# Moving two tiny per-row operations from GpSimd to VectorE in a layer norm with GELU

## The chip, the cores and the metric

The kernel runs on one core of a Trainium2 chip. The metric is the device time of that core in microseconds (us). All runs compared here are of the same state (fast, TensorE clock 1.0 in the profiles).

## The reference

```python
x: (8, 1024, 2048) float32          # 8192 rows of 2048
mean = np.mean(x, axis=-1, keepdims=True)
var = np.var(x, axis=-1, keepdims=True)
normalized = (x - mean) / np.sqrt(var + eps)
out = gamma * normalized + beta
return 0.5 * out * (1 + np.tanh(np.sqrt(2 / np.pi) * (out + 0.044715 * out ** 3)))
```

Input and output are 67.1 MB each, and each has to cross once between HBM (the memory outside the core) and SBUF (the memory that the engines work on).

## The kernel before

A row tile is 128 rows. There are 64 of them, in 16 batches of four. A batch (4.19 MB) is loaded by one DMA into one of five slots, worked on in place, and stored from the same slot by one DMA. A slot is reloaded when its store has landed. The first batch is loaded, and the last one stored, tile by tile. For each tile the engines do this:

- VectorE: four statistics instructions of 512 elements (`bn_stats`), an aggregate (`mvs` = mean and variance), and, for the tile before, the multiplication by gamma (`zg`).
- GpSimd: `ves` = variance + eps, `rss` = ves to the power -1/2, `nms` = -mean * rss.
- ScalarE: `yk` = x * rss + nms, and, for the tile before, GELU out of PSUM (the memory that TensorE sums into) back into the slot.
- TensorE: beta (two rows) plus zg, summed in PSUM.

```python
# GpSimd, per row tile k of a batch
po.tensor_scalar(out=ves[:, c], in0=mvs[:, k, 1:2], scalar1=float(eps), scalar2=1.0,
                 op0=ALU.add, op1=ALU.mult)._wait_ge(s_a, k + 1).then_inc(s_q, 1)
po.tensor_tensor(out=rss[:, c], in0=ves[:, c], in1=mhalf, op=ALU.pow)._wait_ge(s_q, 2 * k + 1).then_inc(s_q, 1)
po.tensor_scalar(out=nms[:, c], in0=mvs[:, k, 0:1], scalar1=rss[:, c], scalar2=-1.0,
                 op0=ALU.mult, op1=ALU.mult)._wait_ge(s_q, 2 * k + 2).then_inc(s_p, 1)
...
# VectorE, per row tile: stats(k), then scale(k - 1)
def stats(s, q, wait, count):
    ...                                   # four bn_stats
    ve.bn_aggr(out=mvs[:, q], in_=sts[:, q])._wait_ge(s_o, count).then_inc(s_a, 1)
def scale(q, count):
    ve.tensor_tensor(out=zgs[q % 2], in0=yks[q % 2], in1=g_t, op=ALU.mult)._wait_ge(s_n, count).then_inc(s_z, 1)
...
# ScalarE, per row tile t: yk(t), then gelu(t - 1); after a batch's last gelu its store
ac.activation(out=yks[t % 2], in_=xts[slot(b)][:, q], func=ACT.Identity, scale=rss[:, q:q + 1],
              bias=nms[:, q:q + 1])._wait_ge(s_p, t + 1).then_inc(s_n, 1)
...
# SyncE: before a slot is loaded again, its store must have landed
sy.wait_ge(s_store[s], stored(b))
```

Of the kernel before, what the change touches and what calls it, by code (L numbers as in the profile page):

```python
# [8 lines left out]
ALU = mybir.AluOpType  # L9

R = 4
SLOTS = 5
# [4 lines left out]
def kernel(  # L17
# [28 lines left out]
    def sb(name, shape, dt):  # L46
        return pool.tile(shape, dt, name=name)
# [13 lines left out]
    sts = sb("sts", [P, R, nsub, nc.vector.BN_STATS_DIM], f32)  # L61
    mvs = sb("mvs", [P, R, 2], f32)
    ves = sb("ves", [P, R], f32)
    rss = sb("rss", [P, R], f32)
    nms = sb("nms", [P, R], f32)

    def sem(name):
        return tc.alloc_semaphore(name)

    s_first = [sem(f"first{q}") for q in range(R)]  # L70
    s_load = [sem(f"load{s}") for s in range(SLOTS)]
# [4 lines left out]
    s_o = sem("o")  # L76
    s_a = sem("a")
    s_z = sem("z")
    s_q = sem("q")
    s_p = sem("p")  # L80
# [7 lines left out]
    def slot(b):  # L88
        return (b + SLOTS - 1) % SLOTS

    def row(p):
        return rows[p:p + 1, :, :d // K]

    def split(v):
        return v.rearrange("o (k f) -> o k f", k=K)
# [10 lines left out]
    with tc.tile_critical(no_gpsimd_drain=True):  # L106
        with nc.Block(no_gpsimd_drain=True) as block:

            @block.sync
            def _(sy):  # L110
                for b in range(B):
                    s = slot(b)
                    if stored(b):
                        sy.wait_ge(s_store[s], stored(b))
                    for q in range(R):
                        if b == 0:
                            sy.dma_start(out=xts[s][:, q:q + 1], in_=xg[0, :, q:q + 1]).then_inc(s_first[q], 16)
                    if b:
                        sy.dma_start(out=xts[s], in_=xg[b]).then_inc(s_load[s], 16)

            @block.gpsimd
            def _(po):
                po.memset(ones, 1.0)  # L123
                po.memset(ones_b, 1.0)
                po.memset(mhalf, -0.5)
                po.memset(ident, 0.0).then_inc(s_setp, 1)
                po.affine_select(out=ident, in_=ident, compare_op=ALU.not_equal, fill=1.0, base=0,  # L127
                                 pattern=[[-1, P]], channel_multiplier=1)._wait_ge(s_setp, 1).then_inc(s_setp, 1)
                with po.Fori(0, B):
                    for k in range(R):  # L130
                        c = slice(k, k + 1)
                        po.tensor_scalar(out=ves[:, c], in0=mvs[:, k, 1:2], scalar1=float(eps), scalar2=1.0,  # L132
                                         op0=ALU.add, op1=ALU.mult)._wait_ge(s_a, k + 1).then_inc(s_q, 1)
                        po.tensor_tensor(out=rss[:, c], in0=ves[:, c], in1=mhalf,  # L134
                                         op=ALU.pow)._wait_ge(s_q, 2 * k + 1).then_inc(s_q, 1)
                        po.tensor_scalar(out=nms[:, c], in0=mvs[:, k, 0:1], scalar1=rss[:, c], scalar2=-1.0,  # L136
                                         op0=ALU.mult, op1=ALU.mult)._wait_ge(s_q, 2 * k + 2).then_inc(s_p, 1)
                    po.sem_inc(s_a, -R)
                    po.sem_inc(s_q, -2 * R)

            @block.vector
            def _(ve):
                def stats(s, q, wait, count):
                    xr = xts[s][:, q].rearrange("p (s f) -> p s f", f=FMAX)
                    for j in range(nsub):
                        ins = ve.bn_stats(out=sts[:, q, j, :], in_=xr[:, j, :])  # L146
                        if j == 0 and wait:
                            ins._wait_ge(*wait)
                            if wait[0] is s_load[s]:
                                ins.then_inc(s_load[s], -16)  # L150
                    ins.then_inc(s_o, 1)
                    ve.bn_aggr(out=mvs[:, q], in_=sts[:, q])._wait_ge(s_o, count).then_inc(s_a, 1)  # L152

                def scale(q, count):
                    ve.tensor_tensor(out=zgs[q % 2], in0=yks[q % 2], in1=g_t,  # L155
                                     op=ALU.mult)._wait_ge(s_n, count).then_inc(s_z, 1)

                ve.memset(b_hl, 0.0).then_inc(s_m, 1)  # L158
                for q in range(R):
                    stats(slot(0), q, (s_first[q], 16), q + 1)  # L160
                    if q == 0:

                        ve.tensor_tensor(out=split(b_hl[32:33]), in0=row(32), in1=split(b_hl[32:33]),  # L163
                                         op=ALU.subtract)._wait_ge(s_c, 2).then_inc(s_m, 1)
                        ve.wait_ge(s_c, 3)
                    else:
                        scale(q - 1, q)
                ve.sem_inc(s_o, -R)
                ve.sem_inc(s_n, -(R - 1))
                with ve.Fori(0, (B - 1) // SLOTS):  # L170
                    for k in range(SLOTS * R):
                        s, q = divmod(k, R)
                        stats(s, q, (s_load[s], 16) if q == 0 else None, k + 1)
                        scale((q - 1) % R, k + 1)
                    ve.sem_inc(s_o, -SLOTS * R)
                    ve.sem_inc(s_n, -SLOTS * R)
                scale(R - 1, 1)

            @block.scalar
# [100 lines left out]
```

## Time and profile before

| | before |
|---|---|
| median time | 319.93 us (319.73 to 319.96, 3 runs) |
| span in the profile | 318.1 us |
| busy: ScalarE, VectorE, TensorE, GpSimd | 251.5, 247.1, 244.4, 110.5 us |
| DMA | 134.26 MB, mean 422 GB/s over the span |

Three compute engines are busy 77 to 79% of the span, and none is full. The view of groups gives, for the lines concerned, the count, the busy time in us and the mean duration of one in ns, then the idle time ahead of them:

```profile
L132 POOL TENSOR_SCALAR ves<-mvs 128x1 f32<-128x1 f32 x64 | 38.4, 600 | 174.1 <-DVE mvs L152 174.1
L155 DVE TENSOR_TENSOR zg<-yk,g_t 128x2048 bf16<-128x2048 bf16 x64 | 76.4, 1194 | 19.4 <-ACT yk L192 19.4
...
L136 POOL TENSOR_SCALAR nms<-mvs,rss 128x1 f32<-128x1 f32 x64 | 35.9, 560 | 6.3
L134 POOL TENSOR_TENSOR rss<-ves,mhalf 128x1 f32<-128x1 f32 x64 | 35.3, 551 | 5.3
```

The means of the first and third hide two cases each, alone and while zg runs: 0.19 and 1.03 us for the addition, 0.27 and 0.88 us for the product (the timeline in the prediction shows all but the 0.27). The idle time of 174.1 us says that GpSimd mostly waits for work. The wait of 19.4 us is VectorE's, for yk, the result that needs the GpSimd chain.

### The profile page before, as it was taken

The numbers are of one execution on the slowest core, as the hardware profiler recorded it, in microseconds if no ns is written. First come the engines' busy times: TensorE is split into PE (matmuls) and PEld (weight loads), VectorE is DVE, ScalarE is ACT, GpSimd is POOL, SyncE is SP. The second block draws the span as 40 slices with busy tenths as digits, with TensorE's granted clock in tenths as the row PEclk, the third lists the DMA queues.
The fourth block names the chain that finished last, engine by engine and source line by source line (L and its number), as shares of the span: only waits on it lengthen the run. The fifth ranks groups of instructions, "written<-read, shape, count | busy, mean of one in ns | idle before, by whom it ended". The sixth has DMA issues, their size and how long they took to land.

```text
span 318.1 us, 2087 instructions
## 1 busy us (share of the span) xinstructions
PE 244.4 (77%) x520; PEld 57.3 (18%) x520; DVE 247.1 (78%) x386; ACT 251.5 (79%) x132; POOL 110.5 (35%) x201
## 2 busy tenths in 40 slices
PE   2769999999999999997868959589595886958810
PEld 1212222222212122221112212112121111211100
DVE  3499999999999999978968699686986869778400
ACT  2669999999999999997967969599595995968820
POOL 1144444444444444443333343342432324423100
DMA  7999999999999999999999999999999999999994
GB/s 292 437 462 396 433 413 408 457 424 433 437 424 445 413 453 424 433 437 424 445 412 457 420 437 433 429 441 416 453 420 441 433 429 441 416 453 412 445 401 205
DMA packets 5570, 134.26 MB, mean 422 GB/s; under 512 B 656, under 2 KB 704, under 8 KB 704
## 3 DMA queue, kind: packets, MB, share of 16 engines
q1 hardware_dynamic: 2736, 67.11, 49.4%
q10 hardware_dynamic: 2832, 67.13, 49.0%
q14 instruction: 2, 0.02, 0.0%
HBM read 67.13 MB, written 67.11 MB: 422 GB/s over the span
## 4 chain that ended last, share of the span: by engine, by line
DMA 45%; DVE 19%; ACT 18%; POOL 9%; PE 3%; issue 2%; ACTq 0%; POOLq 0%; DVEq 0%; SPq 0%
DMA out_dram<-xt 28%; DMA xt<-in_x_dram 15%; ACT yk L192 13%; DVE sts L146 12%; DVE zg L155 5%; POOL ves L132 5%; ACT xt L199 4%; POOL rss L134 3%; PE ps L217 2%; DMA rows<-in_gamma_dram 2%; POOL nms L136 1%; DVE mvs L152 1%; PE ps L234 1%; ACT g_t L188 1%; ACTq L202 0%
## 5 line engine op out<-in xcount | busy, mean ns | idle before, releaser
L146 DVE BATCH_NORM_STATS2 sts<-xt 128x6 f32<-128x512 f32 x256 | 157.7, 678 | 29.2 <-DMA xt<-in_x_dram 27.0
L192 ACT ACTIVATE yk<-xt,nms,rss 128x2048 bf16<-128x2048 f32 x64 | 133.7, 2089 | 44.0 <-POOL nms L136 39.0
L234 PE MATMUL ps<-zg,ident 128*128 128x512 bf16 x256 | 120.8, 628 | 50.7 <-DVE zg L155 49.5
L230 PE MATMUL ps<-b_hl,ones_b 33*128 33x512 bf16 x256 | 120.6, 624 | 2.2 <-PEq L225 2.2
L199 ACT ACTIVATE xt<-ps 128x2048 f32<-128x2048 f32 x64 | 119.0, 1859 | 1.5 <-PE ps L234 1.5
L132 POOL TENSOR_SCALAR ves<-mvs 128x1 f32<-128x1 f32 x64 | 38.4, 600 | 174.1 <-DVE mvs L152 174.1
L155 DVE TENSOR_TENSOR zg<-yk,g_t 128x2048 bf16<-128x2048 bf16 x64 | 76.4, 1194 | 19.4 <-ACT yk L192 19.4
L234 PEld LDWEIGHTS ps<-zg,ident 128*128 128x128 bf16 x256 | 27.8, 131 | 143.8 <-DVE zg L155 108.5
L230 PEld LDWEIGHTS ps<-b_hl,ones_b 33*128 33x128 bf16 x256 | 27.0, 127 | 92.1 <-issue 88.4
L136 POOL TENSOR_SCALAR nms<-mvs,rss 128x1 f32<-128x1 f32 x64 | 35.9, 560 | 6.3
L134 POOL TENSOR_TENSOR rss<-ves,mhalf 128x1 f32<-128x1 f32 x64 | 35.3, 551 | 5.3
L152 DVE BATCH_NORM_AGGREGATE mvs<-sts 128x2 f32<-128x24 f32 x64 | 16.8, 263 | 2.2
L217 PE MATMUL ps<-rows,ones 1*128 1x512 f32 x8 | 7.2, 1076 | 6.0 <-DMA rows<-in_gamma_dram 6.0
L185 ACT ACTIVATE b_hl<-rows 1x2048 bf16<-1x2048 f32 x1 | 1.9, 1908 | 4.8 <-DMA rows<-in_beta_dram 4.8
L217 PEld LDWEIGHTS ps<-rows,ones 1*128 1x128 f32 x8 | 2.5, 325 | 9.1 <-DMA rows<-in_gamma_dram 6.0
L163 DVE TENSOR_TENSOR b_hl<-rows,b_hl 1x2048 bf16<-1x2048 f32 x1 | 2.3, 2281 | 2.2 <-ACT b_hl L186 2.2
L188 ACT ACTIVATE g_t<-ps 128x2048 bf16<-128x2048 f32 x1 | 1.9, 1877 | 2.5 <-PE ps L217 2.5
L181 ACT ACT_TABLE_LOAD x1 | 1.3, 1283 | 0.9 <-SPq L106 0.9
L186 ACT ACTIVATE b_hl<-rows 1x2048 bf16<-1x2048 f32 x1 | 1.9, 1908 | 0.0
L158 DVE MEMSET b_hl<- 33x1024 uint32 x1 | 0.9, 912 | 1.2 <-SPq L106 1.2
L123 POOL MEMSET ones<- 65x128 f32 x1 | 0.2, 201 | 0.5 <-SPq L106 0.5
L127 POOL TENSOR_SCALAR_AFFINE_SELECT ident<-ident 128x128 bf16<-128x128 bf16 x1 | 0.3, 294 | 0.1
(7 smaller groups left out, 0.9 us busy)
## 6 DMA issues: line engine op xcount, KB each, us to landing
xt<-in_x_dram SPq DMA_DIRECT2D x15, 4096.0 KB, 24.8
out_dram<-xt ACTq DMA_DIRECT2D x15, 4096.0 KB, 37.5
xt<-in_x_dram SPq DMA_DIRECT2D x4, 1024.0 KB, 8.2
out_dram<-xt ACTq DMA_DIRECT2D x4, 1024.0 KB, 13.1
rows<-in_beta_dram ACTq DMA_DIRECT2D x2, 8.0 KB, 5.5
rows<-in_gamma_dram ACTq DMA_DIRECT2D x1, 8.0 KB, 5.1
```

Of the source, the lines that this page charges most:

```text
L132: po.tensor_scalar(out=ves[:, c], in0=mvs[:, k, 1:2], scalar1=float(eps), scalar2=1.0, op0=ALU.add, op1=ALU.mult)._wait_ge(s_a, k + 1).the ...
L134: po.tensor_tensor(out=rss[:, c], in0=ves[:, c], in1=mhalf, op=ALU.pow)._wait_ge(s_q, 2 * k + 1).then_inc(s_q, 1)
L136: po.tensor_scalar(out=nms[:, c], in0=mvs[:, k, 0:1], scalar1=rss[:, c], scalar2=-1.0, op0=ALU.mult, op1=ALU.mult)._wait_ge(s_q, 2 * k + 2 ...
L146: ins = ve.bn_stats(out=sts[:, q, j, :], in_=xr[:, j, :])
L152: ve.bn_aggr(out=mvs[:, q], in_=sts[:, q])._wait_ge(s_o, count).then_inc(s_a, 1)
L155: ve.tensor_tensor(out=zgs[q % 2], in0=yks[q % 2], in1=g_t, op=ALU.mult)._wait_ge(s_n, count).then_inc(s_z, 1)
L188: ac.activation(out=g_t, in_=pss[0], func=ACT.Identity)._wait_ge(s_tg, 1).then_inc(s_c, 1)
L192: ac.activation(out=yks[t % 2], in_=xts[slot(b)][:, q], func=ACT.Identity, scale=rss[:, q:q + 1], bias=nms[:, q:q + 1])._wait_ge(s_p, t + ...
L199: ins = ac.activation(out=xt[:, q], in_=pss[i % 2], func=ACT.Gelu_apprx_tanh)._wait_ge(s_t, i + 1)
L217: ins = pe.matmul(pss[0][:, cols(j)], lhsT=ones[64:65], rhs=rows[64:65, j * K // nsub:(j + 1) * K // nsub, :d // K], start=True, stop=True)
L230: ins = pe.matmul(ps[:, cols(j)], lhsT=ones_b, rhs=b_hl[:, cols(j)], start=True, stop=False)
L234: ins = pe.matmul(ps[:, cols(j)], lhsT=ident, rhs=zgs[k % 2][:, cols(j)], start=False, stop=True)
```

## The change

The intent is to shorten the chain from the aggregate to yk: GpSimd keeps only the power. VectorE computes variance + eps right after the aggregate, and -mean/sigma after the first statistics instruction of the next tile, when the power should be done.

```diff
 # GpSimd
-po.tensor_scalar(out=ves[:, c], ... add eps ...)._wait_ge(s_a, k + 1).then_inc(s_q, 1)
 po.tensor_tensor(out=rss[:, c], in0=ves[:, c], in1=mhalf,
-                 op=ALU.pow)._wait_ge(s_q, 2 * k + 1).then_inc(s_q, 1)
-po.tensor_scalar(out=nms[:, c], ... -mean * rss ...)._wait_ge(s_q, 2 * k + 2).then_inc(s_p, 1)
+                 op=ALU.pow)._wait_ge(s_a, k + 1).then_inc(s_q, 1)
 # VectorE, per row tile
 for j in range(nsub):
     ins = ve.bn_stats(out=sts[:, q, j, :], in_=xr[:, j, :])
+    if j == 0 and before is not None:
+        mean(before, count_q)          # nms = -mean * rss of the tile before, waits for the power
-ve.bn_aggr(out=mvs[:, q], in_=sts[:, q])._wait_ge(s_o, count).then_inc(s_a, 1)
+ve.bn_aggr(out=mvs[:, q], in_=sts[:, q])._wait_ge(s_o, count + 1).then_inc(s_o, 1)
+ve.tensor_scalar(out=ves[:, q:q + 1], ... add eps ...)._wait_ge(s_o, count + 2).then_inc(s_a, 1)
 scale(before, ...)                    # zg of the tile before, as it was
 ... (semaphore resets adjusted; ScalarE, TensorE and SyncE unchanged)
```

More of the change, by code (lines that the diff above doesn't have):

```diff
@@ L131, in _, with mean, step @@
                         c = slice(k, k + 1)
-                        po.tensor_scalar(out=ves[:, c], in0=mvs[:, k, 1:2], scalar1=float(eps), scalar2=1.0,
-                                         op0=ALU.add, op1=ALU.mult)._wait_ge(s_a, k + 1).then_inc(s_q, 1)
                         po.tensor_tensor(out=rss[:, c], in0=ves[:, c], in1=mhalf,
-                                         op=ALU.pow)._wait_ge(s_q, 2 * k + 1).then_inc(s_q, 1)
-                        po.tensor_scalar(out=nms[:, c], in0=mvs[:, k, 0:1], scalar1=rss[:, c], scalar2=-1.0,
-                                         op0=ALU.mult, op1=ALU.mult)._wait_ge(s_q, 2 * k + 2).then_inc(s_p, 1)
+                                         op=ALU.pow)._wait_ge(s_a, k + 1).then_inc(s_q, 1)
                     po.sem_inc(s_a, -R)
-                    po.sem_inc(s_q, -2 * R)
             @block.vector
             def _(ve):
-                def stats(s, q, wait, count):
+                def mean(q, count):
+                    c = slice(q, q + 1)
+                    ve.tensor_scalar(out=nms[:, c], in0=mvs[:, q, 0:1], scalar1=rss[:, c], scalar2=-1.0,
+                                     op0=ALU.mult, op1=ALU.mult)._wait_ge(s_q, count).then_inc(s_p, 1)
+                def step(s, q, wait, count, before, count_q, count_n):
                     xr = xts[s][:, q].rearrange("p (s f) -> p s f", f=FMAX)
@@ L146, in stats @@
                         ins = ve.bn_stats(out=sts[:, q, j, :], in_=xr[:, j, :])
-                        if j == 0 and wait:
-                            ins._wait_ge(*wait)
-                            if wait[0] is s_load[s]:
-                                ins.then_inc(s_load[s], -16)
-                    ins.then_inc(s_o, 1)
-                    ve.bn_aggr(out=mvs[:, q], in_=sts[:, q])._wait_ge(s_o, count).then_inc(s_a, 1)
+                        if j == 0:
+                            if wait:
+                                ins._wait_ge(*wait)
+                                if wait[0] is s_load[s]:
+                                    ins.then_inc(s_load[s], -16)
+                            if before is not None:
+                                mean(before, count_q)
+                    ins.then_inc(s_o, 1)
+                    ve.bn_aggr(out=mvs[:, q], in_=sts[:, q])._wait_ge(s_o, count + 1).then_inc(s_o, 1)
+                    ve.tensor_scalar(out=ves[:, q:q + 1], in0=mvs[:, q, 1:2], scalar1=float(eps), scalar2=1.0,
+                                     op0=ALU.add, op1=ALU.mult)._wait_ge(s_o, count + 2).then_inc(s_a, 1)
+                    if count_n:
+                        scale(before, count_n)
                 def scale(q, count):
@@ L159, in _ @@
                 for q in range(R):
-                    stats(slot(0), q, (s_first[q], 16), q + 1)
+                    step(slot(0), q, (s_first[q], 16), 2 * q, q - 1 if q else None, q, q)
                     if q == 0:
@@ L165, in _ @@
                         ve.wait_ge(s_c, 3)
-                    else:
-                        scale(q - 1, q)
-                ve.sem_inc(s_o, -R)
+                ve.sem_inc(s_o, -2 * R)
+                ve.sem_inc(s_q, -(R - 1))
                 ve.sem_inc(s_n, -(R - 1))
@@ L172, in _ @@
                         s, q = divmod(k, R)
-                        stats(s, q, (s_load[s], 16) if q == 0 else None, k + 1)
-                        scale((q - 1) % R, k + 1)
-                    ve.sem_inc(s_o, -SLOTS * R)
+                        step(s, q, (s_load[s], 16) if q == 0 else None, 2 * k, (q - 1) % R, k + 1, k + 1)
+                    ve.sem_inc(s_o, -2 * SLOTS * R)
+                    ve.sem_inc(s_q, -SLOTS * R)
                     ve.sem_inc(s_n, -SLOTS * R)
+                mean(R - 1, 1)
                 scale(R - 1, 1)
```

## The prediction

VectorE's added work: the sum came to 0.27 us per tile (17 us over 64 tiles, 4.03 us a tile, 8.06 us a pair). The durations of the two new operations in it came from no run; what stands of its terms is the 0.08 us by which zg overlaps the aggregate in the trace. So these sums, and the 264 us of VectorE, are forecasts and no measurements. That yk would be there before zg's turn was forecast with the same durations. The sum on the time, 0 us, does not need these terms: it sets the pair's 8.06 or 8.19 us against 9.76 us of DMA at the measured 430 GB/s. The 0.3 us in the sum for the batch boundary agree with the trace, where the product starts 0.30 us before yk (60.80 to 61.10).

> **What bounds the kernel now.** I read the page's busy shares and slices first, because they say whether one resource is full from end to end.
>
> ```profile
> span 318.1 us, 2087 instructions
> ...
> DVE  3499999999999999978968699686986869778400
> ACT  2669999999999999997967969599595995968820
> POOL 1144444444444444443333343342432324423100
> DMA  7999999999999999999999999999999999999994
> ```
>
> Each digit is the busy tenth of a slice of 8 us. VectorE is full only up to slice 17 or so (about 135 us); after that it has holes. The DMA engines are full from the second slice to the last but one. 134.26 MB have to move, and the stretches show at what rate:
>
> ```profile
> 12.00:36.00 24.00, 18.38 (x40) 4.06 (x39) 20.63 (x33) 19.18 (x10) 8.39 (x14) 1.00 1.03 444
> 60.00:130.00 70.00, 63.02 (x137) 14.56 (x136) 64.63 (x104) 64.73 (x35) 30.19 (x54) 1.00 1.00 433
> 205.00:280.00 75.00, 58.67 (x128) 13.68 (x128) 58.10 (x92) 59.49 (x32) 27.23 (x48) 1.00 1.00 433
> 304.00:314.00 10.00, 0.00 (x0) 0.00 (x0) 0.00 (x0) 1.17 (x1) 0.00 (x0) 1.00 0.97 411
> ```
>
> The columns are PE, weight loads, VectorE, ScalarE and GpSimd busy, the clock, the DMA share and GB/s. The rate is 433 both while VectorE is 92% busy (64.63 of 70 us) and while it is 77% busy (58.10 of 75). So compute does not set it. Data flows from about 2 to 314 us: 134.26 MB / 312 us = 430 GB/s. [...]
>
> The second view is who waits in the load queue (SyncE):
>
> ```profile
> SPq L119 <- DMA out_dram<-xt: 246.9, 11, 55.6
> ```
>
> Every reload of a slot waits for the store of that slot. In the timeline the loads from 138 us on are issued every 19.5 us, as are the stores: one batch in and one out, 8.39 MB / 19.5 us = 430 GB/s. A store takes about 44 us from issue to landing then, of which its own data at full rate are only 4.19 MB / 430 GB/s = 9.8 us. The rest is queue. Compute sees the queue as holes: in the waits of VectorE, the statistics waited 27.0 us for loads in 9 waits. The chain of waits, which begins with 130 us of VectorE, GpSimd and ScalarE links, is misleading here. It follows one order of events back, but while it runs through compute the DMA queues have other buffers' work and never empty.
>
> [...]
>
> ```profile
> 58.86 1.16 DVE L155 TENSOR_TENSOR zg<-yk,g_t 128x2048 bf16<-128x2048 bf16 x1
> 59.03 1.03 POOL L132 TENSOR_SCALAR ves<-mvs 128x1 f32<-128x1 f32 x1 [2.63 <-DVE mvs L152]
> ...
> 62.78 0.19 POOL L132 TENSOR_SCALAR ves<-mvs 128x1 f32<-128x1 f32 x1 [1.72 <-DVE mvs L152]
> 63.06 0.55 POOL L134 TENSOR_TENSOR rss<-ves,mhalf 128x1 f32<-128x1 f32 x1
> 63.10 1.85 ACT L199 ACTIVATE xt<-ps 128x2048 f32<-128x2048 f32 x1
> 63.23 1.23 DVE L155 TENSOR_TENSOR zg<-yk,g_t 128x2048 bf16<-128x2048 bf16 x1 [0.53 <-ACT yk L192]
> 63.71 0.88 POOL L136 TENSOR_SCALAR nms<-mvs,rss 128x1 f32<-128x1 f32 x1
> ```
>
> The GpSimd addition takes 0.19 us alone and 1.03 us when the multiplication into zg runs, ending 0.04 us after it. [...]
>
> **The change part by part.** Per row tile (64 of them):
> - Removed from GpSimd: the addition (600 ns mean, 38.4 us in all) and the product (560 ns, 35.9 us). Left is the power, 35.3 us. GpSimd falls from 110.5 to some 36 us if the power never meets zg. It may well meet it, since it now starts when zg starts[...].
> - Added on VectorE: two operations of 128x1. [...] Statistics of 678 ns start every 0.59 us in their groups of four, so neighbours overlap by 0.08 to 0.09 us[...]. The addition waits for the end of the aggregate (263 ns), which today zg overlaps by 0.08 us (66.87 + 0.26 = 67.13 against a start at 67.05). [...] Sum 0.27 us per tile, 17 us over 64 tiles: VectorE goes from 247.1 to about 264 us busy, 83% of the span.
> - The step of compute: today two tiles take 8.19 us (zg starts at 58.86 and 67.05), one step of 3.76 and one of 4.43 us, the longer with a wait of 0.53 us for yk, which came late through three GpSimd operations. With 0.27 added VectorE's own work is 3.76 + 0.27 = 4.03 us a tile. [...] That wait goes. So 8.06 instead of 8.19 us per pair: compute gains 1 to 2% at best.
> - What lies on the path of the end: nothing of this. A tile is 1.05 MB in and 1.05 MB out, so a pair of tiles needs 4.19 MB / 430 GB/s = 9.76 us of DMA. Both 8.06 and 8.19 are below it.
> - The batch boundary: the product of a batch's last tile now stands behind the first statistics of the next batch, so it waits for that load. zg of that tile already stood behind all four statistics, so the store comes only some 0.1 to 0.4 us later: yk is ready at landing + 0.6 + 0.3 + 2.1 = 3.0 us and zg starts then, against 2.7 us today (279.97 to 282.66).
> - The tail, where compute could matter: from 280 us only stores are left. At 288.78, when the last whole-batch store is issued, 10.6 MB are still to be moved (14.37 MB from 280 on by the rates per stretch, less 3.7 to then); 8.39 of them are issued then or later, so 2.2 MB or 5.2 us lie in the queue. At the last store (305.19 us) it is 2.7 MB or 6.2 us ahead of it. A delay of under 1 us is swallowed.
>
> Sum on the time: 0 us, give or take the chance of how loads and stores interleave.
>
> **The rivals.**
> 1. *VectorE becomes the bound.* Its row of slices speaks for it (9 up to 135 us), and 17 us are added to it. Against it: 64 x 4.03 = 258 us plus about 15 us of start is less than 318, and reloads wait for stores, not for compute. If it held, the time would grow by up to 17 us, to 337.
> 2. *A new wait on the power.* If zg blocks the power for its whole run, the power ends at zg's end + 0.55 and the product's turn is at about zg's end + 0.5; with releases VectorE waits 0.1 to 0.2 us a tile. The pair then takes 8.2 to 8.5 us, still below 9.76: no change of the time.
> 3. *The shorter GpSimd chain pays.* The chain of waits has GpSimd at 9% of the span, so someone would hope for a few per cent. If compute bounded, 0.07 us x 64 = 4 us could come off, to 315. Against it is the DMA row.
> 4. *Another interleaving changes the DMA rate.* Slices vary from 396 to 462 GB/s, but long stretches stay within 1% of each other, apart from 414 at 36 to 60 us; shifts of 0.3 us should not move the mean by more than 0.3%.
>
> **Range and chances.** The median before is 319.93 us, with 0.23 us between runs. The expected change is 0; rival 4 gives about 1 us either way, and small misjudged tail effects lean slower. So 319.9 us, range 318.7 to 321.3. Faster by over 2%[...]: 0.01. Slower by over 2% needs rival 1 or a starved queue: 0.02. Within 2%: 0.97.
>
> **What would show it.** In the changed profile: the DMA row still full to the end at 430 GB/s; reloads still waiting for stores, some 247 us; VectorE at about 264 us busy[...]; zg's wait for yk (19.4 us now) mostly gone; in the first 130 us a pair of tiles in 8.0 to 8.4 us; the last store issued within 1 us of 305.2. It would be wrong if slices of the DMA row fell below 9 in the middle, if loads were waited for by a queue that is empty, or if the pair took more than 9.76 us.

## The result, and the profile after

The changed kernel takes **319.63 us** (319.58 to 319.72, 4 runs) against 319.83 us (319.63 to 319.96, 4 runs) for the kernel before on the same chip. The ratio is 0.9995, with a 95% interval of 0.9977 to 1.0012: no change. Ratios here are the mean time of one kernel's fast runs over that of the other's of the same rounds, so not quite the ratio of the medians quoted.

The slices of the changed kernel, as in the prediction:

```profile
span 317.8 us, 2075 instructions
...
DVE  3499999999999999999969799696996969879500
...
POOL 1033323232323231323213222231312213212000
DMA  7999999999999999999999999999999999999994
```

The DMA row is the same digit for digit. VectorE's run of nines has become longer, up to slice 20, and GpSimd is emptier. The stretches, with the same columns as in the prediction (VectorE is the third pair, the last number is GB/s):

```profile
60.00:130.00 70.00, 62.06 (x135) 14.23 (x134) 68.44 (x134) 64.65 (x34) 21.20 (x17) 1.00 1.01 434
...
205.00:280.00 75.00, 58.03 (x126) 13.52 (x127) 63.20 (x124) 60.17 (x32) 19.74 (x16) 1.00 1.00 433
...
304.00:314.00 10.00, 0.00 (x0) 0.00 (x0) 0.00 (x0) 1.29 (x1) 0.00 (x0) 1.00 0.94 399
```

Between 60 and 130 us VectorE went from 64.63 to 68.44 us busy, 98%, and the rate is 434 GB/s, where it was 433. The load queue waits as before:

```profile
SPq L119 <- DMA out_dram<-xt: 247.1, 11, 55.6
```

The groups that changed:

```profile
L132 POOL TENSOR_TENSOR rss<-ves,mhalf 128x1 f32<-128x1 f32 x64 | 78.0, 1219 | 216.5 <-DVE ves L158 157.0
...
L164 DVE TENSOR_TENSOR zg<-yk,g_t 128x2048 bf16<-128x2048 bf16 x64 | 78.0, 1218 | 5.0 <-ACT yk L201 3.0
...
L141 DVE TENSOR_SCALAR nms<-mvs,rss 128x1 f32<-128x1 f32 x64 | 12.6, 196 | 0.0
...
L158 DVE TENSOR_SCALAR ves<-mvs 128x1 f32<-128x1 f32 x64 | 9.8, 154 | 2.2
```

zg's wait for yk fell from 19.4 to 3.0 us. The power's mean rose from 551 to 1219 ns, because it now meets zg in most tiles (about three in four, to judge by 0.55 us alone and 1.46 us with zg). One tile in the timeline of the changed kernel shows both (start and duration in us; the matmuls and ScalarE are left out):

```profile
59.88 1.22 DVE L164 TENSOR_TENSOR zg<-yk,g_t 128x2048 bf16<-128x2048 bf16 x1
60.04 1.46 POOL L132 TENSOR_TENSOR rss<-ves,mhalf 128x1 f32<-128x1 f32 x1 [3.78 <-POOLq L134]
...
61.01 0.69 DVE L148 BATCH_NORM_STATS2 sts<-xt 128x6 f32<-128x512 f32 x1
61.61 0.20 DVE L141 TENSOR_SCALAR nms<-mvs,rss 128x1 f32<-128x1 f32 x1
61.72 1.87 DVE L148 BATCH_NORM_STATS2 sts<-xt 128x6 f32<-128x512 f32 x3
...
63.63 0.26 DVE L157 BATCH_NORM_AGGREGATE mvs<-sts 128x2 f32<-128x24 f32 x1
...
63.93 0.15 DVE L158 TENSOR_SCALAR ves<-mvs 128x1 f32<-128x1 f32 x1
64.00 1.22 DVE L164 TENSOR_TENSOR zg<-yk,g_t 128x2048 bf16<-128x2048 bf16 x1
```

From zg to zg this is 64.00 - 59.88 = 4.12 us, where the kernel before took 8.19 us for two tiles, so 4.095 us for one. Once per batch ScalarE issues a store first, yk is later, and the step is 4.32 us. Over a batch, from the issue of one whole-batch store to the next, the steps are these, first of the kernel before, then of the changed one:

```profile
52.35 0.34 ACTq L207 DMA_DIRECT2D out_dram<-xt  x1
...
68.73 0.34 ACTq L207 DMA_DIRECT2D out_dram<-xt  x1
```

```profile
53.15 0.34 ACTq L216 DMA_DIRECT2D out_dram<-xt  x1
...
69.85 0.34 ACTq L216 DMA_DIRECT2D out_dram<-xt  x1
```

That is 16.38 us before and 16.70 us after. So in its compute the changed kernel is 2% *slower*, and the time does not show it.

### The profile page after: what moved, and what is told of

Same layout as the page of the kernel before. It is cut to its first block, busy times and chain, and to the rows that moved or that the text cites. A ratio compares the mean times of both kernels' runs of the same rounds, so it can differ in the third digit from the quotient of the medians.

```text
span 317.8 us, 2075 instructions
## 1 busy us (share of the span) xinstructions
PE 244.3 (77%) x520; PEld 57.1 (18%) x520; DVE 265.0 (83%) x514; ACT 253.9 (80%) x132; POOL 79.0 (25%) x73
## 4 chain that ended last, share of the span: by engine, by line
DMA 44%; DVE 27%; ACT 19%; PE 3%; issue 2%; ACTq 1%; DVEq 0%; SPq 0%
DMA out_dram<-xt 27%; DVE sts L148 15%; DMA xt<-in_x_dram 15%; ACT yk L201 12%; DVE zg L164 9%; ACT xt L208 7%; PE ps L226 2%; DMA rows<-in_gamma_dram 2%; DVE mvs L157 2%; DVE nms L141 1%; ACTq L216 1%; DVE ves L158 1%; PE ps L243 1%; ACT g_t L197 1%; ACTq L211 0%
## 5 line engine op out<-in xcount | busy, mean ns | idle before, releaser
L148 DVE BATCH_NORM_STATS2 sts<-xt 128x6 f32<-128x512 f32 x256 | 163.5, 681 | 23.7 <-DMA xt<-in_x_dram 21.7
L132 POOL TENSOR_TENSOR rss<-ves,mhalf 128x1 f32<-128x1 f32 x64 | 78.0, 1219 | 216.5 <-DVE ves L158 157.0
L164 DVE TENSOR_TENSOR zg<-yk,g_t 128x2048 bf16<-128x2048 bf16 x64 | 78.0, 1218 | 5.0 <-ACT yk L201 3.0
L141 DVE TENSOR_SCALAR nms<-mvs,rss 128x1 f32<-128x1 f32 x64 | 12.6, 196 | 0.0
L158 DVE TENSOR_SCALAR ves<-mvs 128x1 f32<-128x1 f32 x64 | 9.8, 154 | 2.2
```

Source lines behind the costliest of these rows:

```text
L141: ve.tensor_scalar(out=nms[:, c], in0=mvs[:, q, 0:1], scalar1=rss[:, c], scalar2=-1.0, op0=ALU.mult, op1=ALU.mult)._wait_ge(s_q, count).th ...
L148: ins = ve.bn_stats(out=sts[:, q, j, :], in_=xr[:, j, :])
L158: ve.tensor_scalar(out=ves[:, q:q + 1], in0=mvs[:, q, 1:2], scalar1=float(eps), scalar2=1.0, op0=ALU.add, op1=ALU.mult)._wait_ge(s_o, coun ...
```

## The experiments

The theory: the DMA stream alone sets the time, and compute has room below it. It has three rivals: compute is also on the path, and the change was a wash there (1); the mixing of loads and stores sets the DMA rate (2); the change makes compute faster and only DMA hides it (3). Eight kernels were run. The kernel before took 319.67 us in the first call and 319.75 in the second (7 runs each).

### e1: the DMA stream alone

```diff
-    (GpSimd, VectorE, ScalarE and TensorE programs)
+    # ScalarE only: for each batch, wait for its load, then store it
+    ac.wait_ge(s_load[slot(b)], 16 * (1 + (b - 1) // SLOTS))
+    ac.dma_start(out=og[b], in_=xt).then_inc(s_store[slot(b)], 16)
```

> All loads and stores of the kernel, in the same sizes and on the same two queues, no computation (the result is x, wrong on purpose). Theory (the DMA stream alone sets the end): 134 MB at 430 GB/s is 312 us, plus about 2 us ahead and 4 us behind, so 316 to 320 us, within 1.5% of both kernels. Rival 1 (the chain through VectorE and ScalarE also lies on the path, and the change was a wash there): well below, under 305 us. Rival 2 (the order in which loads and stores mix sets the rate): a time outside 316 to 320 on either side, as the mixing is quite different here.

Measured: 317.66 us, ratio 0.9931 (0.9915 to 0.9948). That is 2 us less than the kernel before. Its stretches (with no other engine at work, the GpSimd pair, the clock, the DMA share and GB/s):

```profile
12.00:36.00 24.00, 0.00 (x0) 1.00 1.02 420
36.00:60.00 24.00, 0.00 (x0) 1.00 1.00 433
60.00:130.00 70.00, 0.00 (x0) 1.00 1.00 434
```

Here each batch is stored as soon as its load has landed, while both kernels load alone up to 36 us, when the first store is issued (at 35.97 and 36.45; 443 or 444 GB/s over 12 to 36 us) and then mix (414 or 415 up to 60). The sums come out nearly the same (424 to 425 GB/s over 2 to 60 us in the kernels, 423 here). Rival 2 falls, as far as one quite different mixing can show it, and rival 1 in its plain form too: with no chain through the engines at all, the time is nearly the same. The 2 us lie at the very end. The full flow stops at about 314 us in all three, but in the two kernels a thin trickle follows: over 314 to 316 us 29 GB/s before and 49 after, at a DMA share of 0.07 and 0.12, which is that of 1.1 and 1.9 of the 16 DMA engines; in e1 it is 4 GB/s. The last store lands at 316.8 us before and 316.5 after; in e1 the rate is 0 from 314.5 us on. Why the trickle follows was not tested.

### e2 and e3: compute laid bare, before and after

Only one row in four of each batch but the last is stored (the outputs are wrong). DMA then needs 87 MB instead of 134.

```diff
-ac.dma_start(out=og[b], in_=xt)._wait_ge(s_r, b + 1).then_inc(s_store[slot(b)], 16)
+ac.dma_start(out=og[b, :, q:q + 1], in_=xt[:, q:q + 1])._wait_ge(s_r, b + 1).then_inc(s_store[slot(b)], 16)
```

> The kernel before, but of each batch except the last only one row in four is stored (wrong on purpose), so DMA has 87 MB, some 203 us, and compute is exposed. Theory: 64 steps of 4.095 us (8.19 us a pair in the trace) + 15 us of start + 16 us of tail = 293 us (288 to 298). If compute were not near its own limit it would fall towards 210 us.

> The same cut of the stores in the changed kernel. Theory: the step is 4.175 us (16.70 us a batch in its trace against 16.38), so 64 x 0.08 = 5 us more than e2_lite_before: ratio 1.015 to 1.02. Rival 1 (compute was a wash): ratio 1.00. Rival 3 (the shorter GpSimd chain helps compute and only DMA hides it): ratio below 0.99.

Measured: 288.70 us for e2, 293.62 us for e3, ratios 0.9032 and 0.9184 to the whole kernel before, so 0.9184 / 0.9032 = **1.017** between them. Both lie in their expected ranges, e2 near the low end of its own. First e2's slices, then e3's:

```profile
DVE  3489999999999999999999999999999999999820
...
DMA  7999999996979797988989895969979230210646
```

```profile
DVE  3499999999999999999999999999999999999930
...
DMA  7999999995979796989989896989696030120656
```

Now it is the DMA row that has holes, and VectorE's that has none. The change makes compute slower by 4.9 us. That is what the batch steps of these two traces give: 16.70 - 16.37 = 0.33 us, over the 15 batches that are stored whole in the full kernel. The steps are those of the full kernels (16.70 and 16.38), so the missing stores did not change the compute. Rivals 1 and 3 fall: the change is neither a wash nor a gain in compute. The room below the DMA stream is then 319.6 - 293.6 = 26 us, or 0.41 us per row tile; e5 and e9 test this figure from both sides.

### e5 and e9: more work on VectorE, with all stores

```diff
 for j in range(nsub):
+    if j == nsub - 1:
+        ve.bn_stats(out=junk, in_=xr[:, 0, :N])     # e5: N = 512, e9: N = 256
     ins = ve.bn_stats(out=sts[:, q, j, :], in_=xr[:, j, :])
```

> The changed kernel with one more statistics instruction of 512 elements per row tile on VectorE (about 0.6 us a tile, 38 us in all), its result unused. Theory: the compute line becomes 64 x 4.775 + 31 = 337 us and is now over the DMA stream, so 332 to 342 us, about half of the added work showing. Rival 1 (compute on the path already): about 358 us. If DMA had slack for everything: 320 us.

> The changed kernel with all stores and one more statistics instruction of 256 elements per row tile. By e5 against e3 the 512 elements added 0.53 us a tile; half of it is 0.27 us, 17 us in all. Theory (exposed compute 293.6 us + 17 = 311 us stays under the DMA stream): 319 to 321 us, ratio to the kernel before 0.998 to 1.005. Rival 1 (compute is on the path): 337 us.

Both are correct. e9: 320.10 us, with three runs at 320.07 to 320.12 and one at 323.5, which nothing here explains and which pulls the ratio to 1.0047 (0.9992 to 1.0102). In its timeline a tile takes 4.45 us (103.09 to 107.54, zg to zg), 0.33 us more than 4.12. But here the tile with the store issue takes no longer, and over a batch the step grows less: 17.79 us (store issues at 108.94 and 126.73) against 16.70, which is 0.27 us a tile, as expected, and some 17 us over 64 tiles on the busiest engine. In three of the four runs this changes the time by under half a microsecond. e5: 327.22 us, ratio 1.0237 (1.0220 to 1.0254). A tile takes 4.71 us there, and the DMA row has its first hole:

```profile
DVE  4599999999999999999999999999999999999950
...
DMA  7999999999999999999999999999999999992797
```

e9's rows, for comparison, still have the DMA row of the two kernels:

```profile
DVE  3599999999999999999999999999998989979710
...
DMA  7999999999999999999999999999999999999994
```

The hole in e5 lies near the end, where only stores are left: from 293 to 301 us the engines move 115 GB/s and from 301 to 303 us nothing, until the last whole-batch store is issued at 302.71 us. So the two limits cross between these doses, added steps of 17 and of 34 us. The expected 332 to 342 us for e5 was too high: I had set 31 us for start and tail, while e3 leaves 293.6 - 64 x 4.175 = 26.4 us, and the step grew by 0.53 to 0.54 us, not 0.6. From e3 and the batch step (18.85 against 16.70 us, 15 times 2.15) one gets 293.6 + 32 = 326 us, close to the 327.2 measured.

### e6 and e7: each half of the change alone, with compute laid bare

```diff
 # e6, on top of e3: the product goes back to GpSimd, behind the power
+po.tensor_scalar(out=nms[:, c], ... -mean * rss ...)._wait_ge(s_q, k + 1).then_inc(s_p, 1)
-            mean(before, count_q)
 # e7, on top of e3: variance + eps goes back to GpSimd, ahead of the power
+po.tensor_scalar(out=ves[:, c], ... add eps ...)._wait_ge(s_a, k + 1).then_inc(s_v, 1)
-ve.tensor_scalar(out=ves[:, q:q + 1], ... add eps ...)
```

> Stores cut as in e2 and e3, and half of the change: only variance + eps moves to VectorE; GpSimd keeps the power and then the product. Theory (VectorE's own order sets the exposed step): VectorE gains 0.19 us a tile but the product is again late behind a power that zg blocks, so some 0.1 to 0.3 us of wait for yk come back: 290 to 300 us. Rival (the two VectorE operations add up and waits don't matter): half to two thirds of the 4.9 us between e2 and e3, 291 to 292 us.

> Stores cut as in e2 and e3, and the other half: only the product moves to VectorE; GpSimd keeps the addition and the power. Theory: the addition is blocked by zg (1.03 us), so the power is ready about 0.2 us after the product's turn and VectorE waits: step about 4.1 to 4.2 us, 289 to 294 us. Rival (costs add, no new wait): 0.13 us a tile on VectorE less the old wait of 0.27 us a tile on average for yk: 280 to 286 us, faster than e2.

Measured: 293.57 us for e6 (ratio 0.9182), 300.82 us for e7 (ratio 0.9411). The effects do not add. Against e2 (288.70) the addition alone costs 4.9 us, the product alone 12.1 us, and both together 4.9 us. e6 lies in its wide range of 290 to 300 us, above the rival's 291 to 292; zg waits there 7.3 us in all for yk, against 19.9 in e2 and 3.0 in e3. That e6 and e3 take the same time was not taken apart further. e7 was outside both expectations. Its timeline shows why:

```profile
99.52 1.23 DVE L166 TENSOR_TENSOR zg<-yk,g_t 128x2048 bf16<-128x2048 bf16 x1
99.53 1.26 POOL L133 TENSOR_SCALAR ves<-mvs 128x1 f32<-128x1 f32 x1 [2.42 <-DVE mvs L161]
...
100.66 0.69 DVE L152 BATCH_NORM_STATS2 sts<-xt 128x6 f32<-128x512 f32 x1
100.87 0.55 POOL L135 TENSOR_TENSOR rss<-ves,mhalf 128x1 f32<-128x1 f32 x1
101.46 0.21 DVE L145 TENSOR_SCALAR nms<-mvs,rss 128x1 f32<-128x1 f32 x1
...
101.71 2.09 ACT L203 ACTIVATE yk<-xt,nms,rss 128x2048 bf16<-128x2048 f32 x1 [0.46 <-DVE nms L145]
...
103.83 1.23 DVE L166 TENSOR_TENSOR zg<-yk,g_t 128x2048 bf16<-128x2048 bf16 x1
```

The GpSimd addition starts as zg does and runs until 100.79 us, 0.04 us after zg ends. The power follows to 101.42, and the product can only start at 101.46, 0.80 us after the statistics instead of 0.60. yk then ends at 103.80, and the next zg starts at 103.83. It is a closed loop of 4.31 us: zg holds up the addition, that the power, the product and yk, and yk the next zg. The addition's mean in e7 is 979 ns, against 0.19 us alone and 1.26 us with zg, so by estimate about three tiles in four are in this loop. The full change leaves it: with the addition on VectorE only the power can meet zg, and it ends in time, as e8 shows.

### e8: does VectorE wait for the power?

```diff
 # on top of e3; wrong results on purpose
-ve.tensor_scalar(out=nms[:, c], ..., scalar1=rss[:, c], ...)._wait_ge(s_q, count).then_inc(s_p, 1)
+ve.tensor_scalar(out=nms[:, c], ..., scalar1=mhalf, ...).then_inc(s_p, 1)
+ve.wait_ge(s_q, count_q)        # moved to just ahead of zg
-ac.activation(out=yks[t % 2], ..., scale=rss[:, q:q + 1], ...)
+ac.activation(out=yks[t % 2], ..., scale=mhalf, ...)
```

> e3 with the product and yk made from a constant instead of the power (wrong on purpose), so that the product waits for nothing; GpSimd still computes the power, which VectorE waits for only ahead of zg, when it is long done. Theory (the product's turn comes when the power is done anyway): within 0.5% of e3. Rival (a new wait on the power, rival 2 of the prediction): 0.1 us a tile less, 287 us or below.

Measured: 294.45 us (ratio 0.9209, against 0.9184 for e3). Freed from the power the kernel is no faster, but 0.3% slower; the extra wait instruction ahead of zg may be the reason, which was not tested. The trace of the changed kernel says the same more directly: the product starts 0.60 us after the statistics whether zg blocked the power (61.01 to 61.61) or not (56.89 to 57.49), and VectorE idles 0.0 us ahead of it (the nms line above). So the blocked power costs nothing that can be seen in the changed kernel.

No run points to a version that beats both kernels by more than the 0.7% between them and bare copying.

## Why the prediction was right

- **The bound.** That DMA sets the time was right for the reason given. e1 confirms it from below (copying alone takes 317.66 us), e9 from above (some 17 us more on VectorE's step do not show). Of the signs, the full DMA row was the one that tells. The reloads that wait for stores are not: the load queue waits just as long in e5 (247.1 us), which compute makes 7.6 us longer, and still 200.2 us in e2, where compute sets the time. The 430 GB/s are a mean and not the most that a stretch shows: the prediction's own first line has 444 over 12 to 36 us, at a DMA share of 1.03. That no higher mean is to be had was not shown.
- **The mark for being wrong was too high.** The prediction would have called itself wrong only if a pair of tiles took more than 9.76 us. In e5 a pair takes 18.85 / 2 = 9.43 us, and the time grows by 7.6 us, because compute also has a start and a tail that DMA does not cover: 26.4 us by e3. With these the mark is, by estimate, (319.6 - 26.4) / 32 = 9.16 us a pair; e9 with 8.89 stays below it.
- **VectorE's busy time.** Predicted about 264 us; 265.0 measured, which is partly luck, as the added work per tile was larger than predicted (next point). Of the two new lines the addition takes 154 and the product 196 ns; why the product takes longer was not tested.
- **The step of compute was mis-sized, with the wrong sign.** The prediction had 0.27 us of added work per tile, 8.06 us per pair, and a gain of 1 to 2%. The added work is 4.12 - 3.76 = 0.36 us. The product with its neighbours costs 0.60 + 0.11 + 1.91 - 2.49 = 0.13 us; 0.05 us more comes from zg, after which the next statistics now start 1.13 instead of 1.08 us later (why was not looked into); the addition costs 0.19 (63.63 to 64.00 is 0.37, against 0.18). The later yk of every fourth tile, behind the issue of a store, was not foreseen either. A pair takes 8.35 us over a batch and compute loses 1.7% (e3 over e2). The time did not depend on it.
- **zg's wait for yk.** Predicted to go almost entirely; it fell from 19.4 to 3.0 us. This was the gain that the change was made for, and the added VectorE work cost more than it gave.
- **Rival 2, a new wait on the power.** Half of it came: zg blocks the power (1.46 instead of 0.55 us), but the power ends 0.40 us after zg and not 0.55 (61.50 against 61.10), just in time for the product. e8 shows no wait. With the addition on GpSimd, in e7, the wait is real and costs 7 us more than the full change.
- **Boundary and tail.** The last whole-batch store is issued at 288.90 us (before: 288.78) and the last store at 305.32 (305.19): 0.1 us later, well within the 5 us that lie in the queue. Behind the last load zg starts 2.99 us after the statistics (280.06 to 283.05), as the predicted 3.0.

## What to carry to other kernels

Look for the resource whose row stays full through stretches in which the engines' load differs, and don't take a chain of waits for the bound when other buffers' transfers fill its time. When a change moves nothing, cut the traffic until the hidden side shows: here that turned "no difference" into "1.7% slower in compute, with 26 us of room". Compare the end of compute, with its start and tail, with the end of the DMA stream, and not only the two steps. And small operations must be judged by what runs on another engine beside them, not alone: here the GpSimd addition took 0.19 us alone and 1.03 or 1.26 us beside zg, the power 0.55 and 1.46, and the two halves of this change cost 4.9 and 12.1 us, and together 4.9.
